# Queries squared into their SBUF tile and scaled out of their PSUM bank, with their rope on GpSimd

## The chip, the cores and the metric

The kernel runs on one core of a Trainium2 chip. The metric is the device time of one execution in microseconds (us). TensorE (PE) multiplies, VectorE (DVE) and ScalarE (ACT) work elementwise out of PSUM and SBUF, GpSimd (POOL) works elementwise out of SBUF alone in this program, and SyncE (SP) issues the transfers. Each engine takes its instructions in the order in which they stand in its own queue, and waits for semaphores of the others.

## The reference

Two layers of a hybrid decoder trunk over 16 meta tokens and 1024 sequence tokens, width 1024, in float32. Each layer normalises its input, multiplies by one wide input projection, and feeds two mixers in parallel: a sliding-window attention with 16 query heads, 2 key/value heads, sinks and partial rotary embedding, and an mLSTM in chunks. Both are gated, concatenated and projected back. What the change touches is the path of the queries:

```python
q = rms_norm(aq.reshape(B, L, ATT_HEADS, ATT_HEAD_DIM), q_norm_g)
q = apply_partial_rope(q, cos, sin)      # on the first 16 of the 64 values of a head
```

A query head of 64 values is divided by the root of its mean square (plus an epsilon), and its first 16 values are turned by position. Gains and the turn are folded into one table (`qrt`).

## The kernel before

Activations lie transposed in SBUF as pairs of high and low parts (`H`), and every projection is three matmuls per pair of parts. Weights come by DMA into `raw`, are copied to their high part by ACT (L159) and subtracted to their low part by POOL (L160) into a ring of eight pairs.

**The queries.** One call of `q_tasks` projects 256 columns (four heads) for all tokens. The 1024 sequence tokens are nine tiles less the meta tile: eight tiles of 128 tokens, two to a PSUM bank of 512 columns, so four banks for each of four groups of heads and each of two layers, 32 banks in all. This text calls the four banks of one group a stretch; there are eight stretches. The banks come from a pool named `pj` with two buffers, which the gate projections (L226 too, `pj<-H,RING`) and the transposes of finished queries (`q_stacks`, L617) also use. A bank takes 48 matmuls. When it is complete, `finish` runs: ACT copies the bank into its place in an SBUF tile `u` (L572) and then squares the bank in place (L573); DVE sums the squares per head out of the bank (L576) and adds the epsilon (L577); POOL raises 8 sums per partition to the power -0.5 (L578). Once two banks, a half of the tokens, are done, `q_post` hands out four pieces: two scalings of the SBUF tile by the result (L541, DVE, 128x512 each) and two pieces of the turn (L551 twice, then L555 and L556, DVE). Then the transposes (L617) may read the tile, and ACT and DVE split them into high and low stacks (L600 to L603) for the scores.

**The attention.** Its steps are s1 (scores into one of two long-lived tiles `S`, L667; mask, maximum, exponential and normalisation, L681 to L693), s2 (transposes of the probabilities into one bank `T`, L704 and L707, evicted by ACT and DVE, L711 to L715, with POOL's mask at L718), s3 and s4 (products into one bank `O`, L731 and L743, evicted at L746 and L748, gated by POOL at L752). `weave` runs these steps between the pieces of a projection: even head pairs go with gate projections, odd ones with the next group's queries. The first stretch of each layer stands ahead of the attention, the other three run inside it, and each stretch is followed by a gate projection.

**The order.** From the first queries on, the matmuls stay in the order in which the program writes them (`pin`). The instructions of the other engines are placed by a list scheduler of the framework, which goes by its own timeline and ranks.

Of the kernel before, what the change touches and what calls it, by code (L numbers as in the profile page):

```python
# [14 lines left out]
AF = mybir.ActivationFunctionType  # L15
ALU = mybir.AluOpType
# [47 lines left out]
def build(ctx, tc, I, O):  # L64
    nc = tc.nc
    ve, sc, gp, pe, sy = nc.vector, nc.scalar, nc.gpsimd, nc.tensor, nc.sync
# [54 lines left out]
    def unit(dt=F32):  # L121
        return up.tile([128, UW], dt, name="u")

    def t384(n=384):
        return tp_.tile([128, 384], F32, name="t")[:, :n]
# [4 lines left out]
    def w1k(dt=F32):  # L130
        return wkp.tile([128, 272], dt, name="w1k")
# [233 lines left out]
    for l in range(DEPTH):  # L365
# [64 lines left out]
        def k_stacks(kv, g, i):  # L430
# [3 lines left out]
            d = 64 - s0 if i else s0  # L434
            hi, lo = [T[d:d + 64, 576 * g:576 * g + 576] for T in Ks]
            sc.activation(hi, src, AF.Copy)
            ve.tensor_tensor(lo, src, Ks[0][s0:s0 + 64, 576 * g:576 * g + 576], op=ALU.subtract)

        def v_stacks(kv, g):

            w = slice(64 * kv, 64 * kv + 64)

            def put(T, src, eng):
                sc.activation(T[:, :, 0:64], src, AF.Copy)
                eng.tensor_tensor(T[:, :, 64:128], src, T[:, :, 0:64], op=ALU.subtract)

# [89 lines left out]

        def q_tasks(m, wgf, st):

            def scale(eng, x4, r):
                p, nt = x4.shape[0], x4.shape[1]  # L540
                eng.tensor_tensor(x4, x4, r.rearrange("p t (v c) -> p t v c", c=1).to_broadcast([p, nt, 4, 64]),  # L541
                                  op=ALU.mult)

            def turn(eng, x4, a, T, part):

                p, nt = x4.shape[0], x4.shape[1]
                T = T[:p, 0:64 * nt].rearrange("p (t v c) -> p t v c", t=nt, v=4)
                tb = qrt[:p, a:a + nt].rearrange("p t (v c) -> p t v c", v=1).to_broadcast([p, nt, 4, 32])
                if part == 0:
                    for i in range(2):  # L550
                        eng.tensor_tensor(T[:, :, :, 8 * i:8 * i + 8], x4[:, :, :, 8 - 8 * i:16 - 8 * i],  # L551
                                          tb[:, :, :, 16 + 8 * i:24 + 8 * i], op=ALU.mult)
                else:
                    x = x4[:, :, :, 0:16]
                    eng.tensor_tensor(x, x, tb[:, :, :, 0:16], op=ALU.mult)  # L555
                    eng.tensor_tensor(x, x, T, op=ALU.add)  # L556

            def finish(ts, ps):
                t, n = ts[-1], 256 * len(ts)
                p = TT[t][1]  # L560
                if ts[0] in (first_q, 1, 5):
                    st["X", t > 4] = unit()
                    if "ss" not in st or t > 4:
                        st["T"] = t384()
                        st["ss"] = sm.tile([128, 2, 5, 4], F32, name="ssq_", bufs=2)
                    if t == 0:
                        st["XM"] = w1k()[:16, 0:256]
                ss = st["ss"]
                i = (ts[0] - 1) % 4 if t else 4
                x = st["XM"] if t == 0 else st["X", t > 4][:, 256 * i:256 * i + n]  # L570
                sq = t384(256)[:p] if t == 0 else ps[:p, 0:n]
                sc.activation(x, ps[:p, 0:n], AF.Copy)  # L572
                sc.activation(sq, ps[:p, 0:n], AF.Square)  # L573
                e = i + len(ts)
                sa, ra = ss[:p, 0, i:e], ss[:p, 1, i:e]
                ve.tensor_reduce(sa, sq.rearrange("p (a c) -> p a c", c=64), axis=mybir.AxisListType.X, op=ALU.add)  # L576
                ve.tensor_scalar(sa, sa, 64.0 * EPS, None, ALU.add)  # L577
                gp.tensor_tensor(ra, sa, nhalf[:p, 0:4 * (e - i)].rearrange("p (t v) -> p t v", v=4), op=ALU.pow)  # L578
                T = st["T"]
                if t == 0:  # L580
                    xm = x.rearrange("p (t v c) -> p t v c", t=1, v=4)
                    scale(gp, xm, ra)
                    for i in range(2):
                        turn(gp, xm, 0, T[:, 256:320], i)
                if t not in (4, 8):
                    return
                x4 = st["X", t > 4][:, 0:1024].rearrange("p (t v c) -> p t v c", t=4, v=4)
                st["post", t > 4] = ([lambda i=i: scale(ve, x4[:, 2 * i:2 * i + 2], ss[:, 1, 2 * i:2 * i + 2])
                                                for i in range(2)] +
                                     [lambda i=i: turn(ve, x4, t - 3, T, i) for i in range(2)])  # L590
            tl = ([[0]] if first_q == 0 else []) + [[1, 2], [3, 4], [5, 6], [7, 8]]
            return [x for ts in tl for x in projN_parts(wgf, ts, 256, lambda ps, ts=ts: finish(ts, ps))]

        def q_post(st, half):

            return [lambda i=i: st["post", half][i]() for i in range(4)]

        def q_put(Q, ps, n):
            Q = Q.rearrange("p (h c) -> p h c", h=2)
# [646 lines left out]
        def turn(least=1):  # L1246
            if len(turns) >= least:
                turns.pop(0)()
# [58 lines left out]
```

## Time and profile before

| | |
|---|---|
| runs | 1952.38 us median of 3 (1951.88 to 1953.71) |
| the profiled execution | 1953.92 us, of which the span of the trace is 1952.2 us |
| PE busy | 1908.1 us of the span (98%) |
| DVE, ACT, POOL busy | 1088.3, 1067.7, 906.4 us |
| granted clock of PE, mean | 0.998 |

A row of a group in the profile reads: line, engine, operation, output tile<-input tiles, shapes, count | busy us, mean ns of one | idle time of the engine just before, and what ended it. A row of a timeline starts with the start and the duration in us. A row of the waits names who waited for whom, the total, the count and the longest. A row of one source line gives minimum/median/maximum in ns, then the first and the last start in us.

### The profile page before, as it was taken

Reading aid. Unit: us, or ns where it says so; the run is one execution under the profiler, and the core shown is the slowest. Engines: PE = TensorE matmul, PEld = TensorE weight load, DVE = VectorE, ACT = ScalarE, POOL = GpSimd, SP = SyncE. Lnnn points to the kernel's source line nnn. Section 1 sums busy time; section 2 is a strip of 40 time slices with the busy share of each in tenths; the row PEclk is TensorE's granted clock in tenths of the full one; section 3 lists DMA queues with packets and bytes.
Section 4 is the critical chain, followed back from the end, with each engine's and each line's share of the span. In section 5 each row is a group of like instructions: output and inputs, shape, how many; then the busy total and the mean of one; then the engine's idle time right before and its main releaser. Section 6 shows DMA issues by size and latency. Waiting matters only on the chain.

```text
span 1952.2 us, 36164 instructions
## 1 busy us (share of the span) xinstructions
PE 1908.1 (98%) x12827; PEld 1799.7 (92%) x12827; DVE 1088.3 (56%) x2966; ACT 1067.7 (55%) x3133; POOL 906.4 (46%) x1102
## 2 busy tenths in 40 slices
PE   8999999999999999999999999999999999999999
PEld 7998898999999999977789999999999999998887
DVE  7777777667454363532445678776673635437211
ACT  6577776747454544643334777776464535446221
POOL 3544544336545454564325345444365444547332
PEclk9999999999999999999999999999999999999999
DMA  4111111121222121455541111112122121226543
GB/s 153 44 37 49 39 43 35 37 65 35 62 60 58 41 56 55 146 164 168 176 132 50 39 37 54 43 36 59 39 58 64 40 67 50 57 62 187 171 149 121
DMA packets 150838, 148.28 MB, mean 76 GB/s; under 512 B 15081, under 2 KB 123921, under 8 KB 150658
## 3 DMA queue, kind: packets, MB, share of 16 engines
q1 hardware_dynamic: 150658, 145.97, 25.5%
q8 instruction: 101, 1.65, 0.4%
q14 instruction: 79, 0.65, 0.1%
HBM read 122.58 MB, written 23.29 MB: 75 GB/s over the span
## 4 chain that ended last, share of the span: by engine, by line
PE 80%; DVE 6%; ACT 4%; issue 3%; POOL 3%; DMA 3%; SPq 0%; POOLq 0%; DVEq 0%; ACTq 0%
PE pj L186 35%; PE pj L226 13%; PE pss L1204 6%; PE pj L1204 6%; PE po L1204 5%; PE po L917 2%; PE S L667 2%; PE pss L917 2%; DMA raw<-in_w_in_dram 2%; PE O L743 2%; POOL RING L160 1%; PE O L731 1%; PE pt L917 1%; ACT t L688 1%; PE T L707 1%
## 5 line engine op out<-in xcount | busy, mean ns | idle before, releaser
L186 PE MATMUL pj<-H,RING 128*128 128x384 f32 (+2 forms) x3456 | 583.0, 322 | 0.0
L186 PEld LDWEIGHTS pj<-H,RING 128*128 128x128 f32 x3456 | 543.3, 188 | 2.5 <-issue 0.2
L160 POOL TENSOR_TENSOR RING<-raw,RING 128x512 fp32r<-128x512 f32 (+1 forms) x192 | 255.5, 1338 | 121.5 <-ACT RING L159 114.4
L226 PE MATMUL pj<-RING,H 128*128 128x256 f32 (+1 forms) x1920 | 268.3, 286 | 3.5 <-DVE u L640 3.5
L226 PEld LDWEIGHTS pj<-RING,H 128*128 128x128 f32 x1920 | 242.5, 189 | 4.0 <-DVE u L640 3.8
L226 PE MATMUL pj<-H,RING 128*128 128x384 f32 (+2 forms) x1152 | 215.0, 326 | 3.9 <-DVE u L603 3.9
L186 PE MATMUL pj<-RING,H 128*128 128x256 f32 x1536 | 209.9, 287 | 3.3 <-DVE H L300 1.6
L178 POOL TENSOR_TENSOR RING<-raw,RING 128x512 fp32r<-128x512 f32 x96 | 125.9, 1318 | 175.8 <-ACT RING L177 167.3
L186 PEld LDWEIGHTS pj<-RING,H 128*128 128x128 f32 x1536 | 193.8, 191 | 6.1 <-DVE H L300 2.1
L226 PEld LDWEIGHTS pj<-H,RING 128*128 128x128 f32 x1152 | 179.4, 189 | 4.8 <-PE T L707 2.3
L177 ACT ACTIVATE RING<-raw 128x512 fp32r<-128x512 f32 x128 | 80.7, 631 | 173.0 <-DMA raw<-in_w_out_dram 139.6
L159 ACT ACTIVATE RING<-raw 128x512 fp32r<-128x512 f32 (+1 forms) x196 | 122.8, 630 | 66.1 <-DMA raw<-in_w_in_dram 50.4
L752 POOL TENSOR_TENSOR u<-u,w1k 128x128 f32<-128x128 f32 (+1 forms) x136 | 63.7, 468 | 172.7 <-DVE w1k L748 168.6
L688 ACT ACTIVATE t<-S,mx 128x145 f32<-128x145 f32 (+1 forms) x272 | 100.3, 373 | 59.8 <-DVE mx L685 52.7
L718 POOL TENSOR_SCALAR_AFFINE_SELECT p<-p 128x512 fp32r<-128x512 f32 x112 | 72.4, 646 | 126.9 <-DVE p L714 126.4
L930 POOL TENSOR_TENSOR p<-u,p 128x258 fp32r<-128x258 f32 x64 | 49.7, 777 | 170.8 <-ACT p L929 155.6
L1204 PE MATMUL pss<-RING,H 128*128 128x512 f32 x384 | 120.5, 394 | 0.0
L1204 PE MATMUL pj<-RING,H 128*128 128x512 f32 x352 | 110.7, 396 | 0.0
L693 ACT ACTIVATE t<-t,mx 128x144 f32<-128x144 f32 (+1 forms) x272 | 97.5, 407 | 20.3 <-DVE mx L690 20.1
L866 DVE SCALAR_TENSOR_TENSOR t<-u,cw,t 128x384 f32<-128x384 f32 (+1 forms) x144 | 107.2, 744 | 2.2
L886 DVE SCALAR_TENSOR_TENSOR t<-t,pj 128x384 f32<-128x384 f32 (+2 forms) x48 | 24.5, 511 | 124.8 <-ACT t L885 124.7
L748 DVE TENSOR_TENSOR w1k<-O,w1k 64x128 f32<-64x128 f32 (+1 forms) x272 | 74.6, 274 | 34.2 <-ACT w1k L746 31.3
(344 smaller groups left out, 3804.6 us busy)
## 6 DMA issues: line engine op xcount, KB each, us to landing
raw<-in_w_out_dram SPq DMA_DIRECT2D x128, 256.0 KB, 2.8
raw<-in_w_in_dram SPq DMA_DIRECT2D x100, 256.0 KB, 2.8
raw<-in_w_in_dram SPq DMA_DIRECT2D x192, 128.0 KB, 2.3
spool<-u SPq DMA_DIRECT2D x56, 192.0 KB, 1.9
p<-x SPq DMA_DIRECT2D x24, 256.0 KB, 3.6
t<-spool SPq DMA_DIRECT2D x30, 192.0 KB, 3.4
p<-spool SPq DMA_DIRECT2D x26, 192.0 KB, 4.2
u<-em SPq DMA_DIRECT2D x8, 576.0 KB, 6.5
```

The costliest lines, as they stand in the source:

```text
L159: sc.activation(hi, raw[:, :, 0:o], AF.Copy)
L160: eng.tensor_tensor(lo, raw[:, :, 0:o], hi, op=ALU.subtract)
L177: sc.activation(hi, raw, AF.Copy)
L178: (ve if i > 8 and i % 2 else gp).tensor_tensor(lo, raw, hi, op=ALU.subtract)
L186: last = pin(pe.matmul(out, a, b, start=(i == 0), stop=(i == n - 1)))
L226: pin(pe.matmul(out(), x, y, start=(k + i == 0), stop=(k == n - 1 and i == 2)))
L688: sc.activation(P[:p, 145 * h:145 * h + 145], S[:p, h, 1 + 127 * h:146 + 127 * h], AF.Exp, bias=mx[:p, 0, h:h + 1], accum_out=mx[:p, 1, h: ...
L693: sc.activation(Pn, Pn, AF.Copy, scale=mx[:p, 2, h:h + 1])
L748: ve.tensor_tensor(y[64 * h:64 * h + 64, :p], O[0:64, p * h:p * h + p], up[0:64, p * h:p * h + p], op=ALU.add)
L866: ve.scalar_tensor_tensor(z, RAW[:, t0 + i:t0 + i + n], wcol(i), z, ALU.mult, ALU.add)
L917: pin(f(*a, **k))
L1204: pin(pe.matmul(ps[:p, :], a, b, start=(i + n == 0), stop=(i == 15 and n == len(terms) - 1)))
```

## The change

- The copy of the bank by ACT is gone. ACT now squares the bank straight into the queries' place in SBUF (L569 of the changed kernel), and DVE sums the squares out of SBUF (L570).
- The scaling reads the bank, and writes the queries over the squares (L573): one DVE instruction for each bank, behind POOL's power, out of `finish`. It was an SBUF to SBUF instruction out of `q_post`. For the meta tile it is on DVE too, where it was on POOL.
- The turn of the eight sequence tiles (L546 twice, L550, L551) is issued on POOL, where it was on DVE. `q_post` hands out two pieces, where it handed out four.

Lines of the old kernel from L600 on stand eight lower in the changed one (L714 is L706 there, L667 is L659).

```diff
-            def scale(eng, x4, r):
-                p, nt = x4.shape[0], x4.shape[1]
-                eng.tensor_tensor(x4, x4, r.rearrange("p t (v c) -> p t v c", c=1).to_broadcast([p, nt, 4, 64]),
-                                  op=ALU.mult)
...
-                sq = t384(256)[:p] if t == 0 else ps[:p, 0:n]
-                sc.activation(x, ps[:p, 0:n], AF.Copy)
-                sc.activation(sq, ps[:p, 0:n], AF.Square)
+                x4, y4 = [y.rearrange("p (t v c) -> p t v c", v=4, c=64) for y in (x, ps[:p, 0:n])]
                 e = i + len(ts)
                 sa, ra = ss[:p, 0, i:e], ss[:p, 1, i:e]
-                ve.tensor_reduce(sa, sq.rearrange("p (a c) -> p a c", c=64), axis=mybir.AxisListType.X, op=ALU.add)
+                sc.activation(x, ps[:p, 0:n], AF.Square)
+                ve.tensor_reduce(sa, x.rearrange("p (a c) -> p a c", c=64), axis=mybir.AxisListType.X, op=ALU.add)
                 ve.tensor_scalar(sa, sa, 64.0 * EPS, None, ALU.add)
                 gp.tensor_tensor(ra, sa, nhalf[:p, 0:4 * (e - i)].rearrange("p (t v) -> p t v", v=4), op=ALU.pow)
+                ve.tensor_tensor(x4, y4, ra.rearrange("p t (v c) -> p t v c", c=1).to_broadcast(list(x4.shape)),
+                                 op=ALU.mult)
                 T = st["T"]
                 if t == 0:
-                    xm = x.rearrange("p (t v c) -> p t v c", t=1, v=4)
-                    scale(gp, xm, ra)
                     for i in range(2):
-                        turn(gp, xm, 0, T[:, 256:320], i)
+                        turn(gp, x4, 0, T[:, 256:320], i)
                 if t not in (4, 8):
                     return
-                x4 = st["X", t > 4][:, 0:1024].rearrange("p (t v c) -> p t v c", t=4, v=4)
-                st["post", t > 4] = ([lambda i=i: scale(ve, x4[:, 2 * i:2 * i + 2], ss[:, 1, 2 * i:2 * i + 2])
-                                                for i in range(2)] +
-                                     [lambda i=i: turn(ve, x4, t - 3, T, i) for i in range(2)])
+                z4 = st["X", t > 4][:, 0:1024].rearrange("p (t v c) -> p t v c", t=4, v=4)
+                st["post", t > 4] = [lambda i=i: turn(gp, z4, t - 3, T, i) for i in range(2)]
...
-            return [lambda i=i: st["post", half][i]() for i in range(4)]
+            return [lambda i=i: st["post", half][i]() for i in range(2)]
```

The order of PE's instructions is the same in both kernels. What releases a bank of queries to PE is now the scaling, where it was the sum of squares. On DVE, at the end of the second layer's last stretch (`ssq` are the sums, `pj` the bank, `S` the scores, `T` the transposed probabilities, `mx` maxima and sums), the old kernel has:

```order
L576 TENSOR_REDUCE ssq__16221<-pj 128x8
L670 COPY S_13187<-snk 128x2
L748 TENSOR_TENSOR w1k<-O,w1k 64x128 x2
L577 TENSOR_SCALAR ssq__16221<-ssq__16221 128x8
L680 MEMSET S_13187 128x2x128
L681 COPY_PREDICATED S_13187<-mask,S_13187 128x2x128
L714 TENSOR_TENSOR p_16415<-T,p_16415 128x256
L715 TENSOR_TENSOR ptm_105<-T,ptm_105 32x128
L685 TENSOR_REDUCE mx<-S_13187 128x2
L541 TENSOR_TENSOR u<-u,ssq__16221 128x512
L748 TENSOR_TENSOR w1k<-O,w1k 64x128 x2
L690 RECIPROCAL mx<-mx 128x2
```

And at the same place of DVE's queue in the changed kernel:

```order
L570 TENSOR_REDUCE ssq__16183<-u 128x8
L740 TENSOR_TENSOR w1k<-O,w1k 64x128 x2
L662 COPY S_13161<-snk 128x2
L571 TENSOR_SCALAR ssq__16183<-ssq__16183 128x8
L672 MEMSET S_13161 128x2x128
L673 COPY_PREDICATED S_13161<-mask,S_13161 128x2x128
L677 TENSOR_REDUCE mx<-S_13161 128x2
L706 TENSOR_TENSOR p_16378<-T,p_16378 128x256
L707 TENSOR_TENSOR ptm_105<-T,ptm_105 32x128
L573 TENSOR_TENSOR u<-pj,ssq__16183 128x512
L682 RECIPROCAL mx<-mx 128x2
L740 TENSOR_TENSOR w1k<-O,w1k 64x128 x2
```

The scaling keeps about its place, behind the eviction of `T` (old L714 and L715, new L706 and L707); the bank, which the first row freed before, is freed by the third row from the end. On POOL, in the first stretch of the second layer (`RING` is the split of the weights, `t` and `u` under L546 to L551 the turn), the old kernel has:

```order
L578 TENSOR_TENSOR ssq__12953<-ssq__12953,cst 128x8
L578 TENSOR_TENSOR ssq__13105<-ssq__13105,cst 128x8
L160 TENSOR_TENSOR RING<-raw,RING 128x2x256 x2
L578 TENSOR_TENSOR ssq__13105<-ssq__13105,cst 128x8
L160 TENSOR_TENSOR RING<-raw,RING 128x2x256 x2
L718 AFFINE_SELECT p_13378<-p_13373 128x512
```

And the changed kernel there:

```order
L572 TENSOR_TENSOR ssq__12929<-ssq__12929,cst 128x8
L546 TENSOR_TENSOR t<-u,qrt 128x16x8 x2
L550 TENSOR_TENSOR u<-u,qrt 128x16x16
L551 TENSOR_TENSOR u<-u,t 128x16x16
L572 TENSOR_TENSOR ssq__13079<-ssq__13079,cst 128x8
L160 TENSOR_TENSOR RING<-raw,RING 128x2x256 x2
L572 TENSOR_TENSOR ssq__13079<-ssq__13079,cst 128x8
L160 TENSOR_TENSOR RING<-raw,RING 128x2x256 x2
L546 TENSOR_TENSOR t<-u,qrt 128x16x8 x2
L550 TENSOR_TENSOR u<-u,qrt 128x16x16
L551 TENSOR_TENSOR u<-u,t 128x16x16
L710 AFFINE_SELECT p_13350<-p_13345 128x512
```

Four instructions of the turn have come between the power of the second bank and that of the third, and four more ahead of the mask of the first probabilities.

## The prediction

> **What bounds the kernel now.** I read the page first, then the busy time of the eight stretches of query projections, then PE's waits there, then the groups and starts of the instructions that the change touches.
>
> ```profile
> span 1952.2 us, 36164 instructions
> PE 1908.1 (98%) x12827; PEld 1799.7 (92%) x12827; DVE 1088.3 (56%) x2966; ACT 1067.7 (55%) x3133; POOL 906.4 (46%) x1102
> ...
> sum 344.00, PE 331.95 PEld 324.37 DVE 268.67 ACT 235.75 POOL 185.79; mean PE 41.49 PEld 40.55 DVE 33.58 ACT 29.47 POOL 23.22
> ```
>
> The third row sums eight windows of 31 to 54 us around the stretches. PE is busy 98% of the span, and nothing in the change alters a matmul or PE's order. So the change can only move the 44.1 us in which PE stands still. In the stretches DVE is the second busiest engine, 268.67 of 344.00 us (78%), and PE already waits for it now and then. These are PE's main waits from 50 to 345 us (first layer), and below the dots from 1040 to 1340 us (second layer):
>
> ```profile
> PE O L731 <- DVE w1k L748: 4.6, 5, 1.7
> PE O L731 <- DVE u L603: 2.5, 4, 1.1
> PE pj L226 <- DVE u L640: 2.4, 2, 1.3
> ...
> PE pj L226 <- DVE u L603: 2.0, 3, 1.1
> PE pj L617 <- DVE u L640: 2.0, 1, 2.0
> PE O L731 <- DVE w1k L748: 1.9, 4, 0.9
> PE T L704 <- DVE ptm L715: 1.6, 2, 1.4
> ```
>
> Together 17.0 us. No wait for a bank of queries (L576) is among them: a bank is squared and summed well before PE comes back to it.
>
> **The work removed and moved.**
>
> ```profile
> L572 ACT ACTIVATE u<-pj 128x512 f32<-128x512 f32 x32 | 19.0, 595 | 14.0 <-PE pj L226 13.9
> L551 DVE TENSOR_TENSOR t<-u,qrt 128x128 f32<-128x128 f32 x32 | 12.6, 430 | 0.3
> L556 DVE TENSOR_TENSOR u<-u,t 128x256 f32<-128x256 f32 x16 | 7.8, 491 | 0.2
> L752 POOL TENSOR_TENSOR u<-u,w1k 128x128 f32<-128x128 f32 x50 | 24.4, 487 | 45.4 <-DVE w1k L748 45.1
> L160 POOL TENSOR_TENSOR RING<-raw,RING 128x512 fp32r<-128x512 f32 (+1 forms) x192 | 255.5, 1338 | 121.5 <-ACT RING L159 114.4
> ```
>
> ACT loses 32 copies, 19.0 us. DVE loses the turn: 12.6 + 7.8 us and sixteen L555 of L556's shape, taken at the same 7.8, so 28 us. POOL gets it: 32 instructions of 128x128 at 0.49 us (L752's shape) and 32 of 128x256, between 0.49 and 1.34 us (L160's shape); by their width I take 0.77. That is 16 + 25 = 41 us on an engine that is busy 185.79 of 344.00 us there. It is off PE's path as long as the turn, 2.5 us in a lump, delays no power and no mask that PE's next product needs. Costed at nothing here; without that cover it is the fourth rival.
>
> The scaling keeps its count and width, but its input comes from PSUM. Its durations and starts now, for the half of the tokens that ends each stretch (the last start is that of the stretch's fourth bank; row three also serves the first bank inside the attention):
>
> ```profile
> L541 DVE TENSOR_TENSOR u<-u,ssq__957 x2: 693/898/1102, 73.5 to 80.2; 128x512 f32<-128x512 f32 x2
> L541 DVE TENSOR_TENSOR u<-u,ssq__1565 x2: 693/746/799, 128.2 to 136.3; 128x512 f32<-128x512 f32 x2
> L541 DVE TENSOR_TENSOR u<-u,ssq__1996 x2: 911/1384/1858, 146.5 to 157.7; 128x512 f32<-128x512 f32 x2
> L541 DVE TENSOR_TENSOR u<-u,ssq__3182 x2: 719/831/943, 228.9 to 244.7; 128x512 f32<-128x512 f32 x2
> L541 DVE TENSOR_TENSOR u<-u,ssq__4354 x2: 915/1304/1692, 309.8 to 321.2; 128x512 f32<-128x512 f32 x2
> L541 DVE TENSOR_TENSOR u<-u,ssq__13105 x2: 692/826/961, 1063.7 to 1071.1; 128x512 f32<-128x512 f32 x2
> L541 DVE TENSOR_TENSOR u<-u,ssq__14057 x2: 691/897/1103, 1133.0 to 1143.4; 128x512 f32<-128x512 f32 x2
> L541 DVE TENSOR_TENSOR u<-u,ssq__15134 x2: 998/1050/1101, 1206.0 to 1218.4; 128x512 f32<-128x512 f32 x2
> L541 DVE TENSOR_TENSOR u<-u,ssq__16221 x2: 854/978/1103, 1279.8 to 1290.6; 128x512 f32<-128x512 f32 x2
> ```
>
> One takes 0.69 us at best and up to 1.86. The mean of these 18 is 0.99 us, 0.30 over the best; over 32, some 10 us. Out of the bank I take 0.69 us for each: the sum of squares over 512 columns, which reads the bank today, takes that (L576 below). So DVE loses about 38 us of its 268.67, a seventh.
>
> [...]
>
> **What is added: the bank is held longer.** Before, a bank was free when its squares were summed. Now it is free when it has been scaled, behind the sum, the epsilon, POOL's power and all that stands ahead of the scaling on DVE. At the end of the second layer's first stretch the chain is bare:
>
> ```profile
> 1065.83 0.60 ACT L572 ACTIVATE u<-pj 128x512 f32<-128x512 f32 x1 [0.48 <-PE pj L226]
> 1066.95 0.69 DVE L576 TENSOR_REDUCE ssq__13105<-pj 128x8 f32<-128x512 f32 x1 [1.17 <-ACT pj L573]
> 1067.68 0.17 DVE L577 TENSOR_SCALAR ssq__13105<-ssq__13105 128x8 f32<-128x8 f32 x1
> 1067.93 1.64 POOL L578 TENSOR_TENSOR ssq__13105<-ssq__13105,cst 128x8 f32<-128x8 f32 x1 [0.48 <-DVE ssq__13105 L577]
> ```
>
> Square 0.60, sum 0.69, epsilon 0.17, power 1.64, scaling 0.69, and hand-overs of about 0.25 together: 4.04 us from the bank's first reader to its release, where the old release came 1.81 us after it (1067.64). PE has two `pj` banks. While one query bank follows another, the next 48 matmuls cover this. At the end of a stretch they don't: a gate projection starts there with only one piece (24 matmuls or fewer) between, and these are the matmuls that now wait for the scaling (first one of each gate projection's bank, in the order of the rows above):
>
> ```profile
> 78.58 0.42 PE L226 MATMUL pj<-H,RING 128*128 128x384 f32 x1
> 157.34 0.34 PE L226 MATMUL pj<-H,RING 128*128 128x384 f32 x1
> 242.80 0.38 PE L226 MATMUL pj<-H,RING 128*128 128x384 f32 x1
> 320.63 0.34 PE L226 MATMUL pj<-H,RING 128*128 128x384 f32 x1
> 1068.85 0.39 PE L226 MATMUL pj<-H,RING 128*128 128x384 f32 x1
> 1141.82 0.34 PE L226 MATMUL pj<-H,RING 128*128 128x384 f32 x1
> 1214.99 0.34 PE L226 MATMUL pj<-H,RING 128*128 128x384 f32 x1
> 1288.56 0.34 PE L226 MATMUL pj<-H,RING 128*128 128x384 f32 x1
> ```
>
> In every case the old scaling started after PE's matmul. I let the new one start where the old one did, less 0.6 us for the copy that is gone, and add 0.69 us and 0.06 us to PE: start + 0.15 - need. That gives 1.77, 0.51, 2.05, 0.72, 2.40, 1.73, 3.56 and 2.19 us, **14.9 us**. From below, the bare chain: from 1065.83 it ends at 1069.87, 1.0 us after 1068.85; if elsewhere nothing queues and the chain fits, 1 us is all there is. From above, no credit for the copy: 8 x 0.6 more, 20 us. I stay near the upper end, because the scaling's place on DVE is fixed by the order, and there it stands behind work that itself comes late from PE. The last stretch shows it:
>
> ```profile
> 1288.17 0.65 ACT L159 ACTIVATE RING<-raw 128x528 fp32r<-128x528 f32 x1 [1.53 <-DMA raw<-in_w_in_dram]
> ...
> 1289.46 0.43 DVE L714 TENSOR_TENSOR p<-T,p 128x256 fp32r<-128x256 f32 x1 [1.57 <-ACT ptm L712]
> ```
>
> There L714 waits for ACT, and ACT had waited for a weight's DMA. The scaling follows L714 and L715 in both orders, so it can't start before 1289.9 (1289.46 + 0.43), whatever the power does; queued behind the waiting L573 are the evictions L748 and L690, for which PE's next O and T wait.
>
> Ten transposes of finished queries (L617) also take a `pj` bank just scaled. The first and the last of them:
>
> ```profile
> 127.83 0.27 PE L617 MATMUL pj<-cst,u 128*128 128x128 f32 x1
> ...
> 1279.43 0.60 PE L617 MATMUL pj<-cst,u 128*128 128x128 f32 x4
> ```
>
> By the same formula they wait 128.2 + 0.15 - 127.83 = 0.5 and 1279.8 + 0.15 - 1279.43 = 0.5 us. At 0.4 each, **4 us**; from below 0, from above (no credit for the copy) 11 us.
>
> **What is given back.** With a seventh of DVE's work gone and ACT 19.0 us lighter, PE's old waits for them shrink. Part of them falls right behind a stretch, where the turn stood on DVE, and a stall of PE also lets DVE catch up. I take half of the 17.0 us, **8.5 us**; the bounds are nothing and all of it.
>
> The sum: 14.9 + 4 - 8.5 = 10.4 us. The profiled execution's span of 1952.2 us becomes 1962.6, and with 1.7 us around it (1953.92 - 1952.2) 1964.3. Its time lies 1.5 us over the median of the runs, so the median goes from 1952.4 to **1962.8 us**, 0.5% slower. Nothing later absorbs it, since PE sets the end.
>
> **The rivals.**
>
> *The relief wins (faster).* The place is DVE's queue inside the attention. If its lag sets PE's waits, 38 us less work ends two thirds of them, 11 us, and the scalings move forward until only the bare chain is left, 1 us at four of the eight ends. Then 4 - 11 = -7 us, 1945 us. It decides as soon as the old waits that end exceed the new stalls. For it speaks DVE's 78%; against it the order, which leaves L714 and L748 ahead of the scaling.
>
> *They balance.* The new stalls are half as long, 7.5 + 2 us, because DVE is earlier as a whole, and 8.5 us are given back: +1 us, 1953.4 us.
>
> *The power is late.* POOL's queue holds weight splits of 1.34 us that wait for DMA and ACT. For the stalls to be set by POOL, the split must stand ahead of the power. At 1.34 us more at half of the 18 places: 10.4 + 12 = 22 us, 1975 us.
>
> *The turn blocks POOL.* 2.5 us in front of the mask L718, whose product PE takes next. One us at each of 12 turns inside the attention: 22 us, too. No wait of PE for L718 is among its rows today, which speaks against it.
>
> That the change doesn't do what it says is excluded by the built order: PE's first matmuls on these banks wait for the scaling.
>
> **How the numbers follow.** The forecast (slower by 4 to 18 us) gets 0.63, balance 0.17, faster 0.10, the two late POOL cases together 0.10. The range of 8 in 10 takes the forecast, most of balance and the near half of POOL's cases: 1950 to 1973 us. A measurement here tells 0.2%, 3.9 us, from no change. Faster by more: 0.10, within: 0.17, slower: 0.73.
>
> **What would show it.** PE's waits in the changed kernel should have rows of L226 and L617 waiting for DVE's scaling (u, L573), eight of 0.5 to 3.6 us before gate projections and some of about 0.5 us, together near 19 us, and the old rows should have fallen to some 9 us. The scaling should take 0.69 us throughout, L546 to L551 on POOL 2.5 us a lump. The prediction is wrong if PE waits for the scaling less than 8 us in all, or if its waits for L748, L715 and L640 don't shrink, or if PE waits for POOL.

## The result, and the profile after

The changed kernel takes 1966.70 us (median of 4 runs, 1964.33 to 1967.74) where the kernel before takes 1952.13 (1950.79 to 1953.71): a ratio of 1.0059, 95% interval 1.0048 to 1.0071. It is slower by 14.6 us. The forecast was 1962.8 us, slower, within 1950 to 1973. The profiled execution's span went from 1952.2 to 1964.5 us. Two lines of the changed kernel's page, and the sum over the same eight windows as before:

```profile
span 1964.5 us, 36118 instructions
PE 1911.7 (97%) x12827; PEld 1803.2 (92%) x12827; DVE 1061.1 (54%) x2906; ACT 1052.4 (54%) x3097; POOL 938.3 (48%) x1162
...
sum 344.00, PE 323.70 PEld 316.41 DVE 242.90 ACT 222.61 POOL 209.72; mean PE 40.46 PEld 39.55 DVE 30.36 ACT 27.83 POOL 26.21
```

The rows that the change removes and moves came out as costed: 28.5 us of turn left DVE, its 32 scalings went from 31.9 to 22.0 us, ACT's copies are gone, and POOL has the turn. The engines as a whole moved less than the prediction took: DVE is busy 27.2 us less in the span, not 38, ACT 15.3 us less, not 19, and POOL 31.9 us more, not 41. (A busy time counts overlapping instructions once, and other rows changed too; the meta tile's scaling, for one, went from POOL to DVE.) PE has 8.3 us less in the same 344 us, so it stands still longer there, though the windows don't hold quite the same work, since the changed kernel runs up to 15 us later in them. PE also has 3.6 us more work in all for the same 12827 matmuls; that is a second cost, told below.

PE's main waits in the changed kernel, from 50 to 345 us and, below the dots, from 1040 to 1340 us:

```profile
PE pj L226 <- DVE u L573: 5.0, 3, 1.8
PE pj L226 <- DVE u L632: 2.4, 2, 1.2
PE pj L226 <- DVE S L668: 1.5, 1, 1.5
PE pj L609 <- DVE u L573: 1.4, 2, 1.1
PE O L723 <- DVE S L668: 1.2, 1, 1.2
PE O L723 <- DVE u L595: 1.0, 4, 0.3
PE pj L226 <- DVE u L595: 0.9, 2, 0.5
...
PE pj L226 <- DVE u L573: 9.2, 5, 3.8
PE pj L609 <- DVE u L573: 1.9, 3, 0.9
PE T L696 <- DVE ptm L707: 1.3, 1, 1.3
PE pj L609 <- DVE u L632: 1.1, 1, 1.1
PE pj L226 <- DVE u L595: 0.5, 1, 0.5
```

The rows with L573 are new: PE waits for the scaling out of the bank, 14.2 us before projections and 3.3 us before transposes. Most other rows are old waits that became shorter. Matmul by matmul, the 21 waits behind the prediction's seven rows went from 17.0 to 7.5 us. The row of `O` for L748 (L740 here) is gone, but its longest wait is not: the matmul that waited 1.69 us for it in before waits 1.19 us here, under the name of L668. No row names POOL.

The gate projection's first matmul at the end of each of the eight stretches, in the changed kernel's timeline, with its wait in brackets:

```profile
80.53 0.42 PE L226 MATMUL pj<-H,RING 128*128 128x384 f32 x1 [1.46 <-DVE S L668]
158.36 0.44 PE L226 MATMUL pj<-H,RING 128*128 128x384 f32 x1 [1.42 <-DVE u L573]
242.98 0.45 PE L226 MATMUL pj<-H,RING 128*128 128x384 f32 x1 [1.78 <-DVE u L573]
321.50 0.44 PE L226 MATMUL pj<-H,RING 128*128 128x384 f32 x1 [1.85 <-DVE u L573]
1073.88 0.41 PE L226 MATMUL pj<-H,RING 128*128 128x384 f32 x1 [1.47 <-DVE u L573]
1148.41 0.45 PE L226 MATMUL pj<-H,RING 128*128 128x384 f32 x1 [1.62 <-DVE u L573]
1225.70 0.69 PE L226 MATMUL pj<-H,RING 128*128 128x384 f32 x1 [3.84 <-DVE u L573]
1303.50 0.44 PE L226 MATMUL pj<-H,RING 128*128 128x384 f32 x1 [2.05 <-DVE u L573]
```

The eight waits make 15.5 us (the first is put down to L668, which came last by the records, and it is the same bank's wait). In the trace of before, each of these matmuls started with no wait.

The moved and changed work, in the changed kernel: three groups of the turn on POOL, the square on ACT, and for one tile the scaling (its durations in ns, shortest, median and longest):

```profile
L546 POOL TENSOR_TENSOR t<-u,qrt 128x128 f32<-128x128 f32 x32 | 14.8, 485 | 2.7 <-DVE u L573 1.8 <-ACT u L428 0.9
L551 POOL TENSOR_TENSOR u<-u,t 128x256 f32<-128x256 f32 x16 | 12.3, 767 | 0.9
L550 POOL TENSOR_TENSOR u<-u,qrt 128x256 f32<-128x256 f32 x16 | 12.2, 766 | 0.5
L569 ACT ACTIVATE u<-pj 128x512 f32<-128x512 f32 x32 | 19.0, 594 | 15.5 <-PE pj L226 15.2
...
L573 DVE TENSOR_TENSOR u<-pj,ssq__1986 x2: 658/674/691, 145.7 to 157.6; 128x512 f32<-128x512 f32 x2
```

The turn costs POOL 39.3 us and 2.5 us a lump. All 32 scalings out of the bank take 0.66 to 0.69 us, as these two do; POOL works beside 24 of them (with the turn beside one).

To account for the rest, PE's idle time ahead of every matmul was worked out from the two traces, matmul by matmul (PE's order is the same in all kernels here), and summed over the two attention parts of the program, 40 to 350 and 1040 to 1310 us by before's clock. "New" is idle that grew, "gone" is idle that shrank, "rest" is what matmuls themselves took more or less. All in us:

| kernel | new | gone | rest | sum |
|---|---|---|---|---|
| changed kernel | +19.9 | -13.5 | +4.8 | +11.2 |

Outside these parts the profiled execution lost 1.1 us more in all; one wait at 934.8 us, at the layer's norm, is alone 2.2 us longer (2.42 us in before, 4.60 in the changed kernel). So the spans are 12.3 us apart. The medians are 14.6 apart, because the profiled execution of before lay 1.8 us above its median and that of the changed kernel 0.5 below.

**The rest: matmuls at half clock.** The granted clock of PE around three of the waits, in the changed kernel's windows (the number behind the five engines is the clock):

```profile
313.00:340.00 27.00, 24.67 (x170) 23.83 (x169) 17.66 (x53) 16.74 (x58) 13.86 (x19) 0.94 0.21 55
1143.00:1158.00 15.00, 13.38 (x86) 13.07 (x85) 9.14 (x27) 8.41 (x28) 9.13 (x13) 0.89 0.28 79
1221.00:1233.00 12.00, 8.16 (x40) 7.87 (x39) 4.96 (x15) 5.54 (x20) 9.05 (x13) 0.72 0.31 83
```

A finer window shows what the means are made of: from 324 to 325 us the clock is 0.50.

```profile
324.00:325.00 1.00, 1.00 (x5) 1.00 (x4) 0.73 (x3) 0.49 (x2) 0.00 (x0) 0.50 0.87 232
```

At the waits of 1.85, 1.62 and 3.84 us, PE goes to half clock for 3.41, 3.41 and 6.83 us. PE was busy for 12.2 us of these periods, which loses 6.1 us of work. Before has one such period in these parts, at 239.2 us, which loses 1.7 and which the changed kernel hasn't. So half clock makes 4.4 of the 4.8 us.

### The profile page after: what moved, and what is told of

Same layout as the page of the kernel before. It is cut to its first block, busy times and chain, and to the rows that moved or that the text cites. A ratio compares the mean times of both kernels' runs of the same rounds, so it can differ in the third digit from the quotient of the medians.

```text
span 1964.5 us, 36118 instructions
## 1 busy us (share of the span) xinstructions
PE 1911.7 (97%) x12827; PEld 1803.2 (92%) x12827; DVE 1061.1 (54%) x2906; ACT 1052.4 (54%) x3097; POOL 938.3 (48%) x1162
## 3 DMA queue, kind: packets, MB, share of 16 engines
q8 instruction: 101, 1.65, 0.4%
## 4 chain that ended last, share of the span: by engine, by line
PE 82%; DVE 4%; DMA 3%; ACT 3%; issue 3%; POOL 3%; SPq 0%; POOLq 0%; ACTq 0%; DVEq 0%
PE pj L186 34%; PE pj L226 17%; PE pss L1196 6%; PE pj L1196 6%; PE po L1196 5%; PE S L659 3%; PE po L909 2%; PE pss L909 2%; PE O L735 2%; DMA raw<-in_w_in_dram 2%; POOL RING L160 1%; PE O L723 1%; PE pt L909 1%; PE T L699 1%; PE pj L210 1%
## 5 line engine op out<-in xcount | busy, mean ns | idle before, releaser
L226 PE MATMUL pj<-RING,H 128*128 128x256 f32 (+1 forms) x1920 | 268.8, 286 | 4.3 <-DVE u L632 3.4
L226 PEld LDWEIGHTS pj<-RING,H 128*128 128x128 f32 x1920 | 242.6, 189 | 5.2 <-DVE u L632 3.7
L226 PE MATMUL pj<-H,RING 128*128 128x384 f32 (+2 forms) x1152 | 218.5, 330 | 16.9 <-DVE u L573 14.0
L226 PEld LDWEIGHTS pj<-H,RING 128*128 128x128 f32 x1152 | 181.9, 191 | 19.1 <-DVE u L573 13.7
L740 DVE TENSOR_TENSOR w1k<-O,w1k 64x128 f32<-64x128 f32 (+1 forms) x272 | 74.6, 274 | 40.4 <-ACT w1k L738 37.9
L1196 PE MATMUL po<-RING,H 128*128 128x512 f32 x288 | 92.3, 402 | 0.0
```

Source lines behind the costliest of these rows:

```text
L226: pin(pe.matmul(out(), x, y, start=(k + i == 0), stop=(k == n - 1 and i == 2)))
L740: ve.tensor_tensor(y[64 * h:64 * h + 64, :p], O[0:64, p * h:p * h + p], up[0:64, p * h:p * h + p], op=ALU.add)
L1196: pin(pe.matmul(ps[:p, :], a, b, start=(i + n == 0), stop=(i == 15 and n == len(terms) - 1)))
```

## The experiments

The reference runs of before beside them had medians of 1951.9 to 1954.0 us; each ratio is against those on its own chip. The same account as above, for all runs:

| run | median us | ratio (95%) | new | gone | rest | sum |
|---|---|---|---|---|---|---|
| e1 turn alone on GpSimd | 1943.86 | 0.9955 (0.9942 to 0.9968) | +1.4 | -8.6 | -1.3 | -8.5 |
| e2 scaling alone out of the bank | 1957.97 | 1.0026 (1.0015 to 1.0037) | +16.3 | -13.6 | +1.7 | +4.4 |
| e3 fourth bank the old way | 1947.27 | 0.9974 (0.9964 to 0.9984) | +6.6 | -11.8 | -1.6 | -6.8 |
| e4 no wait for the power | 1937.85 | 0.9922 (0.9908 to 0.9936) | +2.1 | -14.2 | -4.4 | -16.4 |
| e5 scaling with priority | 1964.64 | 1.0063 (1.0049 to 1.0076) | +19.9 | -13.3 | +0.7 | +7.2 |
| e6 scaling and turn on GpSimd | 1943.28 | 0.9956 (0.9944 to 0.9969) | +2.9 | -10.4 | -3.1 | -10.6 |
| e7 power twice | 2046.20 | 1.0480 (1.0466 to 1.0495) | +77.8 | -15.7 | +31.6 | +93.6 |
| e8 third and fourth bank the old way | 1944.87 | 0.9962 (0.9949 to 0.9974) | +2.2 | -10.3 | -0.4 | -8.6 |
| e9 first two banks only, turn on VectorE | 1953.21 | 0.9996 (0.9986 to 1.0005) | +4.5 | -3.7 | -0.3 | +0.5 |
| e10 e2 with the power twice | 2050.70 | 1.0491 (1.0473 to 1.0508) | +79.4 | -15.4 | +35.4 | +99.4 |
| e11 e8 with the old way's scaling on GpSimd | 1942.96 | 0.9945 (0.9931 to 0.9960) | +3.8 | -12.3 | -2.3 | -10.8 |
| e12 e4 with the turn on VectorE | 1943.94 | 0.9949 (0.9935 to 0.9963) | +4.6 | -10.8 | -2.9 | -9.1 |

Two things make most of the rest. One is half clock: e3, e4, e6, e9, e11 and e12 avoid the one period that before has in these parts (1.7 us), e1, e5 and e8 have one as before does, the others have more. The other is that a matmul with a wait ahead of it is recorded as some 0.23 us longer than the same matmul without (in the five runs with over ten new waits the median is 0.23 to 0.26 us): in e4 17 matmuls lose their wait and are 3.2 us shorter together. With both, the rest of e4, e6 and e12 comes out within 0.2 us; in e9 1 us stays open. The new, gone and rest of a run are those of one execution.

### The two halves of the change, each alone

e1 is the kernel before with the turn moved:

```
-  [lambda i=i: turn(ve, x4, t - 3, T, i) for i in range(2)]
+  [lambda i=i: turn(gp, x4, t - 3, T, i) for i in range(2)]
```

> The kernel before with one edit: the turn of the queries is issued on POOL; copy, square and scaling stay as they were, so a bank is free once its squares are summed. My theory (the longer hold of the banks costs some 19 us plus a few of slower clock, and the work taken from DVE gives back about 15): PE waits for no scaling, and its old waits for DVE fall by most of what the turn's 28 us bring. Expected 1941 to 1947 us, 5 to 11 under the kernel before. Rival (the turn's 41 us on POOL hold up powers and masks, and the relief in the changed kernel came from the copy that is gone): 1951 us or more, with PE waits that end on POOL or on evictions behind it.

e2 is the changed kernel with the opposite edit, turn(gp, z4, ...) back to turn(ve, z4, ...).

> The changed kernel with the turn put back on DVE: only the squaring into SBUF and the scaling out of the bank are left. My theory: the same waits for the scaling, 17 to 22 us, and less relief, since DVE keeps the turn: 1966 to 1974 us, at or above the changed kernel. Rival (the loss comes from the turn on POOL): about the kernel before, 1950 to 1955 us.

Measured: the turn alone gains, 1943.86 us, inside what was expected. The scaling alone costs 6 us, 1957.97, and was expected at 1966 or more: a miss. PE's waits in e1 and, below the dots, in e2, over the whole span:

```profile
PE T L704 <- DVE ptm L715: 4.0, 3, 1.7
PE O L731 <- DVE w1k L748: 2.8, 4, 1.0
...
PE pj L226 <- DVE u L573: 12.7, 8, 3.8
PE pj L609 <- DVE u L573: 1.3, 2, 1.0
```

So one half gains 8, the other loses 6, and together they lose 14.6: some 17 us are lost between them. The account has 15.3 of them. Relief is had only once, 8.7 us: e1 frees 8.6, e2 13.6, both together 13.5 instead of 22.2. New idle is 2.2 us more than the two alone make (19.9 against 16.3 and 1.4), and the rest 4.4 us more (4.8 against 1.7 and -1.3), most of it half clock. This last part is the least certain, since it differs between executions (e5 below).

### Is it the ends?

e3 keeps copy, square in the bank and scaling from SBUF for the fourth bank of each stretch, with the turn on GpSimd:

```
+ old = t == 8
+ sq = ps[:p, 0:n] if old else x
+ if old:
+     sc.activation(x, ps[:p, 0:n], AF.Copy)
  sc.activation(sq, ps[:p, 0:n], AF.Square)
  ...
- ve.tensor_tensor(x4, y4, ra..., op=ALU.mult)
+ ve.tensor_tensor(x4, x4 if old else y4, ra..., op=ALU.mult)
```

> The changed kernel, but in the fourth bank of each of the eight stretches (token tiles 7 and 8) ACT copies the bank out and squares it in place, and the scaling reads SBUF, as before; the other three banks of a stretch are scaled out of the bank. My theory (the ends of the stretches carry three quarters of the new waits): the waits of the gate projections for the scaling vanish, some 14 to 16 us with the clock's share; 1948 to 1954 us. Rival (a wait that ends there comes back at the next bank or eviction, since DVE is what lags): 1960 to 1967 us.

Measured: 1947.27 us, 19 us less than the changed kernel, 0.7 below what was expected. All eight waits of the gate projections at the ends are gone; most of what is left of the holds stands before transposes (lines from L577 on are 4 higher here than in the changed kernel):

```profile
PE pj L613 <- DVE u L577: 3.8, 5, 1.2
```

e8 is the same with `old = t in (6, 8)`, so the third bank too, which stands ahead of most of those transposes.

> The changed kernel with the third and fourth bank of each stretch by copy, square and scaling in SBUF as before; the first and second are scaled out of their bank. Hold theory (only a bank whose next user stands close behind is paid for: the gate's first tile behind the fourth, the transposes behind the third and once behind the first): of the 6.6 us of new idle in the run with the fourth bank alone by the old way some 1.5 to 3 stay, and of the 11.8 us relief some 9 to 11: 1941 to 1945. Rival, holds cost everywhere (banks are handed on in a ring, so any hold comes out later): 1946 to 1950, as with the fourth alone.

Measured: 1944.87 us, inside what was expected. Of the waits before transposes one of 0.31 us is left, at 209.6 us by before's clock, and new idle goes from 6.6 to 2.2. The first and second bank are still scaled out of their place, and that is worth nothing beside e1: 0.9962 against 0.9955, intervals overlapping. A hold costs only where the bank's next user stands close behind.

### What the hold consists of

e4 multiplies by the sums in place of the power, so the scaling no longer waits for POOL:

```
- ve.tensor_tensor(x4, y4, ra.rearrange(...).to_broadcast(...), op=ALU.mult)
+ ve.tensor_tensor(x4, y4, sa.rearrange(...).to_broadcast(...), op=ALU.mult)
```

> The changed kernel, but the scaling multiplies by the sums of squares themselves and not by POOL's power of them; the power is still computed and nothing reads it, so the queries are scaled wrongly. The wait for POOL between sum and scaling, 1.9 us, is gone from the hold, and the scheduler puts the scaling ahead of the eviction of T at the ends of the stretches. My theory (the hold is what costs): waits for the scaling fall to 5 us or less, 1948 to 1956 us. Rival (the hold doesn't matter, ACT's and DVE's queues ahead of the square and the sum do): within 3 us of the changed kernel.

Measured: 1937.85 us, 10 us below the expected range. The mechanism is the expected one, the size is not: new idle falls to 2.1 us, the relief stays at 14.2 though of the eight waits at the ends only one is left (0.85 us at the seventh), and no half-clock period is left but the one behind the last matmuls (mean granted clock 1.000). In the changed kernel the end at 1148 us shows both parts of the hold. First the power in POOL's timeline, then two lines of DVE's:

```profile
1144.80 1.64 POOL L572 TENSOR_TENSOR ssq__14027<-ssq__14027,cst 128x8 f32<-128x8 f32 x1
...
1146.90 0.42 DVE L706 TENSOR_TENSOR p<-T,p 128x256 fp32r<-128x256 f32 x1 [0.90 <-ACT ptm L704]
1147.67 0.69 DVE L573 TENSOR_TENSOR u<-pj,ssq__14027 128x512 f32<-128x512 f32 x1
```

The power is done at 1146.44, but the scaling starts at 1147.67: it stands behind the eviction of `T` (L706, L707), which waited 0.90 us for ACT. In e4, without the power, the order puts the scaling ahead of that eviction, so e4 takes away both parts at once. From the square's end to the scaling's end the eight ends take 3.78, 4.84, 6.70, 5.28, 3.90, 5.42, 5.93 and 5.87 us, 41.7 in all; eight bare chains of 3.44 (the 4.04 of the prediction less the square) would take 27.5. So 14.2 us are queueing, on DVE mostly. At the longest wait, 3.84 us, POOL has a part:

```profile
1221.65 1.26 POOL L160 TENSOR_TENSOR RING<-raw,RING 128x512 fp32r<-128x512 f32 x1
1222.88 0.45 POOL L744 TENSOR_TENSOR u<-u,w1k 128x128 f32<-128x128 f32 x1
1223.29 1.63 POOL L572 TENSOR_TENSOR ssq__15100<-ssq__15100,cst 128x8 f32<-128x8 f32 x1
```

The sums were ready at 1221.72 (L571), the power started at 1223.29 behind a weight's split and a gating product. At the other seven ends it starts 0.08 to 0.35 us after the sums. e2 has the same wait, 3.85 us, so the turn is not its cause.

e5 tried to take the queueing away:

```
+ with tc.high_priority(offset=EARLY):
      ve.tensor_reduce(sa, ...); ve.tensor_scalar(sa, ...); gp.tensor_tensor(ra, ...); ve.tensor_tensor(x4, y4, ...)
```

> The changed kernel with one thing more: sum, addition, power and scaling of a bank are placed ahead of other work whose turn has come on VectorE and GpSimd, by the priority that the kernel gives other steps. Hold theory (the idle of TensorE at the ends is the time from the end of the square to the end of the scaling, and what of it is not the chain itself is work that stands ahead in VectorE's order): in the changed kernel's trace that time is 3.8 to 6.7 us at the eight ends where the chain with nothing between takes 3.4; of the 15.5 us of idle at the ends some 10 to 12 go, and the periods at half clock with them, so about 1949, 1946 to 1955. Rival, fixed chain (the crossing between the three engines is what takes the time): no difference, 1963 to 1969. Rival, pushed work (what stands ahead now is the eviction that TensorE needs next): the waits turn up again behind the evictions of the scores, 1960 to 1968.

Measured: 1964.64 us, as the rival "fixed chain" had it, but it is no test of it. The order of all queues came out as in the changed kernel, but for three pairs of neighbouring rows on VectorE. So whether an earlier place would shorten the waits stays untried. The run is of use in another way: it is the changed kernel's order executed again. Its waits are the same within 0.11 us at each of the eight ends, 19.9 us new in both, but the rest is +0.7 in place of +4.8. The same three places in e5's windows:

```profile
313.00:340.00 27.00, 24.69 (x183) 23.83 (x182) 18.47 (x57) 18.31 (x64) 13.89 (x19) 1.00 0.21 55
1140.00:1155.00 15.00, 13.42 (x96) 13.11 (x96) 9.25 (x29) 9.62 (x33) 8.97 (x12) 1.00 0.24 68
1216.00:1228.00 12.00, 8.15 (x45) 7.87 (x44) 5.32 (x17) 5.76 (x21) 8.94 (x14) 0.86 0.31 82
```

Behind the same waits of 1.84 and 1.58 us the clock stayed at 1.00 here, and behind the 3.85 us it was halved for one period instead of two.

e7 lengthens the hold instead; the power is issued twice, and nothing is left out:

```
  gp.tensor_tensor(ra, sa, nhalf..., op=ALU.pow)
+ gp.tensor_tensor(ra, sa, nhalf..., op=ALU.pow)
```

> The changed kernel with the power issued twice, the second over the first with the same value: the hold of every bank is longer by one power, 1.65 us, and nothing else is. Hold theory: the 13 waits for the scaling grow by that, 13 x 1.65 = 21 us, some of the other 19 banks begin to be waited for, and the idle times of over 3 us bring more periods at half clock (3.4 us each, so 1.7 us lost): 1988 to 2008. Rival, VectorE's order sets the moment of the scaling and the power is hidden beside it: 1966 to 1976.

Measured: 2046.20 us, 80 more than the changed kernel, and 38 more than the upper expectation. The direction is the hold theory's; the size needs three terms. The order puts other work between the two powers. POOL's timeline at the sixth end, and under the dots DVE's:

```profile
1200.55 1.64 POOL L572 TENSOR_TENSOR ssq__14053<-ssq__14053,cst 128x8 f32<-128x8 f32 x1
1202.15 0.46 POOL L745 TENSOR_TENSOR u<-u,w1k 128x128 f32<-128x128 f32 x1
1202.57 1.27 POOL L160 TENSOR_TENSOR RING<-raw,RING 128x512 fp32r<-128x512 f32 x1
1203.79 0.65 POOL L711 TENSOR_SCALAR_AFFINE_SELECT p<-p 128x512 fp32r<-128x512 f32 x1
1204.40 1.64 POOL L573 TENSOR_TENSOR ssq__14053<-ssq__14053,cst 128x8 f32<-128x8 f32 x1
...
1206.07 0.69 DVE L574 TENSOR_TENSOR u<-pj,ssq__14053 128x512 f32<-128x512 f32 x1 [2.65 <-POOL ssq__14053 L573]
```

Here the hold grows by 3.85 us (from the first power's start to the second's), not by 1.65. Second, the waits go from 13 to 20. Third, the rest, nearly all half clock, is 31.6 us (mean granted clock 0.979, where the changed kernel has 0.996). PE's waits for the scaling, over the whole span:

```profile
PE pj L226 <- DVE u L574: 46.4, 10, 6.8
PE pj L610 <- DVE u L574: 19.8, 10, 2.7
```

e10 does the same to e2, to see whether the turn on GpSimd made the 80 us:

> The run with the scaling alone (turn on VectorE) with the power issued twice. It splits the 80 us that the second power cost beside a turn on GpSimd. Theory that GpSimd's queue made most of it (the second power, 53 us in all, meets the turn's 39 us there, and the power is issued late): here the hold grows by 1.65 us alone, the 13 to 20 waits by 21 to 33, and periods at half clock add 5 to 15, so 1984 to 2006. Rival, the turn has no part in it (the hold itself, more waits and the half clock make it): about 80 us more here too, 2028 to 2045.

Measured: 2050.70 us, the rival's side, and 6 us above its range: the second power costs no less with the turn on VectorE, 93 us over e2 (new idle 79.4 beside 77.8 in e7). That GpSimd's queue is crowded by the turn falls; what stands between the powers is weight splits, masks and gating products, which GpSimd has in both.

### Why the two reliefs don't add

The waits that e1 removes or shortens stand at 13 matmuls, 11 of them in the 16 us behind the ends, where the turn stood on DVE. e2, which leaves it there, removes the same ones. Two explanations: less work on DVE of either kind ends them, or in e2 the stall just ahead lets DVE catch up. e9 scales only the first two banks out of their place, with no stall at the ends and the turn on VectorE (e8 with turn(ve, z4, ...)):

> The kernel before with one part of the change on half of the banks: the first and second bank of each stretch are scaled out of their bank, the third and fourth as before, and the turn stays on VectorE. Overlap theory (the scaling out of the bank does free VectorE time for TensorE's old waits, and it is the same waits that the turn on GpSimd frees): with one or two short new waits of 0.3 to 0.6 us, and a relief of 3 to 6 us, 1946 to 1950. Rival, swallowed waits (the 13.6 us relief in the run with the scaling alone was for the most part old waits that vanish because a new stall stands just ahead of them, and the scaling by itself frees little): without the stalls there is no relief, 1950.5 to 1953.5.

Measured: 0.9996 (0.9986 to 1.0005), no difference, as the rival had it. PE's waits from 40 to 345 us in e9 and, under the dots, in e1 (lines from L577 on are 4 lower in e9):

```profile
PE O L727 <- DVE w1k L744: 4.4, 5, 1.7
PE pj L226 <- DVE u L599: 2.2, 2, 1.1
...
PE O L731 <- ACT t L693: 1.8, 1, 1.8
PE O L731 <- DVE w1k L748: 1.8, 3, 0.7
PE pj L226 <- DVE u L603: 0.9, 2, 0.4
```

The longest wait of e9's first row (1.7 us) has not gone in e1: it stands in the row of L693, at the same matmul. The shorter ones went. The first two banks cost as much as they free (4.5 and 3.7 us). For the other two, e12 is e4 with the turn on VectorE, so all banks are scaled out of place and hardly a stall is left at the ends:

> The run without the wait for the power, with the turn back on VectorE: the banks are scaled out of the bank by their sums instead of by the power (the queries come out wrongly scaled; the power is computed and not read), so no stall stands at the ends. Open is why the old waits behind the ends (13 places between 85.8 and 1303.4 us, 7 us in all) vanish both where the turn is on GpSimd and where the banks alone are scaled out of place. Overlap theory (less VectorE work, whichever, ends them): they are gone here too, new idle about 2 us, relief 13 to 14, 1938 to 1942. Rival, swallowed waits (with the turn on VectorE they vanish only behind a stall, in which VectorE catches up): with no stall they stay, the relief is 7 us, 1944 to 1949.

Measured: 1943.94 us, at the edge of the rival's range; the account says it is some of both. One stall of 0.59 us is left at the seventh end. At the 13 matmuls before waits 10.8 us in all, e9 10.3, e12 6.6, e1 3.4 and e2 2.7. At one more, at 1145.2 us, before waits 0.24 us, e9 0.90, e12 1.95 and the others not at all. One of the 13, 1.07 us in before and nothing in e1 and e2, is this in e12:

```profile
158.34 0.47 PE L723 MATMUL O<-p,u 128*128 128x256 f32 x2 [1.55 <-ACT ptm L704]
```

So of the 8 us that e2 frees there, 2.5 to 4 come without a stall (with and without the place at 1145.2 us), and 4 to 6 only where a stall stands, which hands the time over rather than saves it. With the turn on GpSimd hardly a stall is needed: e1 has its relief with none at the ends, e4 with one of 0.85 us. e12 also lacks the wait for the power and has another order on DVE, so the split is rough, and that the stall is what frees the rest is argued, not shown.

### A version that beats both

e6 leaves the bank as before and gives GpSimd scaling and turn (`scale(gp, ...)`, `turn(gp, ...)`):

> The kernel before (copy and square out of the bank) with scaling and turn both on GpSimd, so that power, scaling and turn of a half follow each other there. Relief theory (the turn on GpSimd and the scaling out of the bank free the same VectorE time, so the second frees no more; without a hold nothing is paid for it): VectorE loses the turn and the 32 scalings, TensorE's old waits shrink as far as in the run that scales out of the bank, by 13 us instead of 9, and no bank is held: 1937 to 1942. Rival, late GpSimd (scaling adds 1.3 us a bank there, as a product of 16x256 took 0.60 us, and the next power stands behind it): TensorE waits for the queries, 1946 to 1965.

Measured: 1943.28 us, 1.3 above the expected range: with turn and scalings off DVE 10.4 us of waits are freed, not 13. e11 is e8 with the third and fourth bank's scaling on GpSimd:

```
- ve.tensor_tensor(x4, x4 if old else y4, ra..., op=ALU.mult)
+ (gp if old else ve).tensor_tensor(x4, x4 if old else y4, ra..., op=ALU.mult)
```

> Turn on GpSimd; the first and second bank of each stretch scaled out of their bank by VectorE, the third and fourth copied, squared and then scaled by GpSimd in SBUF. Relief theory: no bank with a user close behind is held, and VectorE has the least work of all runs, so the relief of the runs with half of the banks (10 us) grows by 1 to 3: 1940 to 1944. Rival, late GpSimd (a scaling there stands ahead of the next power and the turn): 1945 to 1950.

Measured: 1942.96 us, as expected, 0.9945 (0.9931 to 0.9960). e1, e6, e8 and e11 can't be told apart by their intervals. All are 0.4 to 0.5% faster than the kernel before and 1% faster than the changed one, and e1 is the smallest edit: the turn on GpSimd, and nothing else of the change.

## Why the prediction was right, term by term

**The ends: 14.9 us, measured 15.5.** Place by place the formula gave 1.77, 0.51, 2.05, 0.72, 2.40, 1.73, 3.56 and 2.19 us; the waits are 1.46, 1.42, 1.78, 1.85, 1.47, 1.62, 3.84 and 2.05. Letting the new scaling start where the old one stood in the order was the step that carried this. Its one real miss is the second and fourth end (0.5 and 0.7 forecast, 1.4 and 1.85 measured). e3 shows that these eight are what costs.

**The transposes: 4 us, measured 3.3.** Right in size; five of the ten wait, not all.

**The relief: 8.5 us, measured 13.5.** This term was mis-sized, and in its base more than in its share. "I take half of the 17.0 us" was a choice without a row, and the 17.0 us were 21 of the 29 waits over 0.15 us that before has from 50 to 345 and from 1040 to 1340 us, 22.5 us together. The 21 fell by 9.5 us, near the half. The eight that the prediction left out fell by 3.5 more, such as the transposes' at 71.8 us (0.59 us) and the scores' at 85.8 us (0.64), both gone. The waits didn't fall alike: L748's went from 6.5 to 1.2 us, L715's went from 2.5 to 1.8 us, and L226's for L640 stayed at 2.4, where the prediction had named L640 among those that must shrink. It is not the stalls that free the time in the changed kernel: e4 has 14.2 us of it with one stall of 0.85 us. And it came with less taken from DVE than the prediction had, 27.2 us of busy time in place of 38.

**The rest: not foreseen, 4.8 us.** The sum had no term for what a wait does to the matmuls behind it, and half clock is 4.4 of these. Before's own trace had the warning: a clock of 0.97 in the window from 198 to 252 us, behind a wait of 1.69 us. A last 1.1 us of new idle stands at other matmuls. The two errors, 5.0 us of relief and 4.8 us of rest, cancel, and that is luck: in e5, the same order executed again, the rest is 0.7 us. The forecast of +10.4 us beside +14.6 in the medians is better than its terms.

**Costed at nothing, and found so.** The turn on POOL: 39.3 us against 41 estimated, 2.5 us a lump, no row of PE waiting for POOL in the two views of its waits. The scaling's 0.69 us: 0.66 to 0.69 in all 32, beside POOL's work (24 of them) and without it. With both inputs in SBUF the same product took 0.67 to 0.69 us in before at the nine places where GpSimd did nothing beside it, and 0.69 to 3.45 at the other 23; in e1, with the turn on GpSimd, 0.67 to 3.44 over all.

**The rivals.** "The relief wins" had the turn's half right: alone it gains 8 us, and the ends take it back. "The power is late" is seen at one end of eight, where a weight's split stands ahead of it, and there in e2 as well. "The turn blocks POOL" falls with e1. "They balance" fell short by the clock and by the ends.

## What to carry to other kernels

A PSUM bank that is read once more at the end of a chain over three engines is held for the whole chain and for whatever stands ahead of its last step in the queue (3.78 to 6.70 us here from the square's end, where the bare chain has 3.44): count which users of the ring of banks stand close behind, since only they pay (going back to the old way for eight of 32 banks took 19 us off here). Gains of two edits that relieve the same waits didn't add (8.6 and 13.6 us alone, 13.5 together), so time each half alone; here one half was worth 0.45% and the other was a loss. Where TensorE sets the end, a new wait can cost more than itself: behind the waits of 1.62, 1.85 and 3.84 us matmuls ran at half clock for 3.41, 3.41 and 6.83 us here, which lost 6.1 us of work.

## What was unexpected of the hardware

Over the 14 traces of this study, the first 20 and the last 15 us left out, none of TensorE's 153 idle times of 1.0 to 1.6 us was followed by a half-clock period; of those of 1.6 to 2.1 us 13 of 45 were, of 2.1 to 3.4 us 13 of 25, and of more than 3.4 us all 23. In the traces of before and of the changed kernel alone it is none of 23, 3 of 8, the one of its kind, and both. Every period lasted 3.41 us or two or three times that, at 0.50, and none came without such an idle time ahead of it. The same idle time at the same place was followed by one in one execution and not in the other (1.85 us in the changed kernel's trace, 1.84 in e5's), and the rest of the two executions is 4.8 and 0.7 us, so about 4 us differ between these two.

The starts of the periods in the changed kernel's trace are at 323.09, 937.49, 1149.12 and 1224.21 us, which is 180, 62 and 22 times 3.413 us from one to the next; in before they are at 239.17 and 935.49 us, 204 times that. In the 3.413 us ahead of these six starts TensorE was busy for 1.60, 0.00, 1.79 and 1.06 us, and for 0.84 and 0.99 us in before. Cut into steps of 3.413 us from these starts, the two traces have 1112 other steps at full clock, in which it was busy for 1.58 us or more, in all but three for over 1.8. The wait of 1.62 us at the sixth end, with half clock behind it, fell into one step. That of 2.05 us at the eighth, with none, fell into two (1.27 and 0.78 us), which had 2.14 and 2.63 us busy. But the wait of 1.78 us at the third end left 1.63 us busy in its step, less than the 1.79 at the sixth, and no half clock came behind it. So what decides behind a short wait is not shown.
